# Moving one half-tile load from the sync queue to the queue of ScalarE, beside the end of a store

## The chip, the cores and the metric

The kernel runs on one core of a Trainium2 chip. The metric is the device time in microseconds of one execution. "Span" is the time from the first to the last instruction in the profile of one execution; in every timed execution below, the time is 1.7 to 1.9 us more than its span.

## The reference

It is a rotary position embedding on half of each head. `x` is 16 x 512 x 16 x 64 in float32 (33.55 MB); `cos` and `sin` are 512 x 32.

```python
x1, x2 = (x[..., :half_dim], x[..., half_dim:])          # half_dim = 32
rotated_first  = x1[..., :16] * cos[..., :16] - x1[..., 16:] * sin[..., :16]
rotated_second = x1[..., :16] * sin[..., :16] + x1[..., 16:] * cos[..., :16]
return np.concatenate([rotated_first, rotated_second, x2], axis=-1)
```

Each byte of `x` comes in once and goes out once: 67.1 MB in all.

## The kernel before

The tensor is cut into T = 4 tiles of 8.39 MB. A tile has 64 KB in each of 128 partitions, in a ring of three slots, so tile 3 must wait until tile 0 has been stored. VectorE rotates each tile in place in two halves.

```python
    ring = const_pool.tile([P, NS, K, H, D], fp32)      # NS = 3 slots, K = 16 rows of a tile per partition
    ...
    load(0)
    load(1)
    load(2, 0, KC)                                      # KC = 8: half of tile 2
    ...
    def rotate(t, lo, hi):                              # four VectorE operations: mul, mul, sub, add
        ...
    def turn(t):
        rotate(t, 0, KC)
        rotate(t, KC, K)
        return store(t)

    turn(0)                                             # rotates tile 0 and stores it
    load(2, KC, K)                                      # the other half of tile 2, behind that store
    near = load(3, 0, KL)                               # KL = 14 of 16; waits for the store to land
    load(3, KL, K)
    tc.add_manual_dep(turn(1).ins, near.ins.name, ...)  # the store of tile 1 waits for the near load
    turn(2)
    turn(3)
```

All of these transfers are issued on the sync queue (`nc.sync`). In what follows the "near load" is the first load of tile 3, the "moved load" the second half of tile 2, and a "row" the part of a transfer that lies in one partition: 64 KB for a full tile, 32 KB for a half.

## Time and profile before

| | before |
|---|---|
| time, median of the first 3 runs | 161.47 us (161.44 to 161.71) |
| span of the profiled run | 160.3 us |
| VectorE busy | 112.4 us (70%) |
| DMA engines busy | 97.8% of the span |
| bytes moved | 67.24 MB, 433 GB/s from 24 to 150 us |
| store of tile 0 issued / landed | 49.94 / 72.5 us |
| moved load issued / landed | 50.33 / 81.9 us |
| store of tile 1 issued | 98.96 us |

A DMA that is issued is not yet at work: the 16 DMA engines take its rows after those of the DMAs ahead. The page's section 6 tells the time from issue to landing. What holds an issue back stands in the waits of the sync queue (SPq). The profiled execution took 162.1 us, 0.6 more than the median of the timed ones; a second profile of the same kernel (before_again below, 161.64 us) has the store landed at 71.8 and the store of tile 1 issued at 98.47.

### The profile page before, as it was taken

To read this page: it belongs to the slowest core of one execution; us is meant where nothing else is said; L and a number is where in the kernel's file an instruction comes from. 1 tells how busy PE (TensorE), PEld (TensorE's weight loads), DVE (VectorE), ACT (ScalarE), POOL (GpSimd) and SP (SyncE) were. 2 spreads that over 40 slices of the span, in tenths; PEclk is the share of its full clock that TensorE was granted. 3 is DMA by queue.
4 is the path that set the end of the run, shared out by engine and by line. 5 is a ranking of instruction groups with operands and counts; after the bars stand their busy time and mean duration, and the time that the engine had idled before them with its cause. 6 is when DMAs were issued, how large, how long until landed. Compare 5 with 4: busy or idle time off the path is not lost.

```text
span 160.3 us, 113 instructions
## 1 busy us (share of the span) xinstructions
DVE 112.4 (70%) x43; POOL 1.4 (1%) x6
## 2 busy tenths in 40 slices
DVE  1000959999999999999999999999999950000000
POOL 3000000000000000000000000000000000000000
DMA  7969969699699996999999995996996996996990
GB/s 262 540 262 540 491 294 523 278 507 491 294 392 441 474 523 262 523 392 392 499 482 458 458 444 253 546 523 262 523 523 262 523 507 278 523 507 278 523 507 16
DMA packets 1504, 67.24 MB, mean 419 GB/s; under 512 B 192, under 2 KB 192, under 8 KB 224
## 3 DMA queue, kind: packets, MB, share of 16 engines
q1 hardware_dynamic: 1440, 67.11, 97.6%
q0 software_dynamic: 64, 0.13, 0.2%
HBM read 33.69 MB, written 33.55 MB: 419 GB/s over the span
## 4 chain that ended last, share of the span: by engine, by line
DVE 59%; DMA 14%; issue 7%; DVEq 1%
DVE b_t L96 22%; DVE ring L97 22%; DMA ring<-in_x_dram 14%; DVE ring L101 10%; DVE ring L98 4%; DVEq L148 1%; DVEq L96 0%
## 5 line engine op out<-in xcount | busy, mean ns | idle before, releaser
L96 DVE TENSOR_TENSOR b_t<-ring,table 128x4096 f32<-128x4096 f32 x8 | 35.5, 4432 | 2.1 <-DMA ring<-in_x_dram 1.9
L97 DVE TENSOR_TENSOR ring<-ring,table 128x4096 f32<-128x4096 f32 x8 | 35.4, 4424 | 0.3
L98 DVE TENSOR_TENSOR ring<-ring,b_t 128x2048 f32<-128x2048 f32 x8 | 18.3, 2287 | 0.3
L101 DVE TENSOR_TENSOR ring<-ring,b_t 128x2048 f32<-128x2048 f32 x8 | 18.2, 2280 | 0.0
L73 DVE LOAD_MASK_SELECT spun<-stage x1 | 0.0, 14 | 14.4 <-DMA stage<-in_sin_dram 14.4
L83 DVE COPY table<-packed 32x1024 f32<-32x1024 f32 x4 | 2.7, 684 | 0.1
L80 DVE COPY packed<-spun 32x512 f32<-32x512 f32 (+3 forms) x4 | 1.7, 416 | 0.1
L61 DVE MEMSET stage<- 128x512 f32 x1 | 0.5, 485 | 0.9 <-PEq L137 0.9
L73 DVE STREAM_SHUFFLE spun<-stage 128x512 f32<-128x512 f32 x1 | 0.7, 723 | 0.0
L63 POOL DMA_DIRECT2D stage<-in_cos_dram x1 | 0.6, 649 | 1.3 <-DVE stage L61 1.3
L64 POOL DMA_DIRECT2D stage<-in_sin_dram x1 | 0.5, 532 | 0.0
L137 POOL MEMSET const-float32-0.0<- 128x1 f32 x1 | 0.1, 93 | 0.2 <-issue 0.2
L137 POOL MEMSET const-bfloat16-1.0<- 128x1 bf16 x1 | 0.1, 95 | 0.0
L137 POOL MEMSET const-uint8-127<- 128x1 uint8 x1 | 0.1, 93 | 0.0
L137 POOL MEMSET const-float32-1.0<- 128x1 f32 x1 | 0.1, 92 | 0.0
## 6 DMA issues: line engine op xcount, KB each, us to landing
ring<-in_x_dram SPq DMA_DIRECT2D x2, 4096.0 KB, 41.4
ring<-in_x_dram SPq DMA_DIRECT2D x1, 7168.0 KB, 26.4
ring<-in_x_dram SPq DMA_DIRECT2D x1, 1024.0 KB, 28.5
stage<-in_cos_dram POOLq DMA_DIRECT2D x1, 64.0 KB, 9.0
stage<-in_sin_dram POOLq DMA_DIRECT2D x1, 64.0 KB, 13.4
out_dram<-ring SPq DMA_DIRECT2D x4, 25.6
ring<-in_x_dram SPq DMA_DIRECT2D x2, 32.0
```

The lines of the kernel that those rows point to most:

```text
L61: nc.vector.memset(stage[:, :, :, 0:Q], 0.0)
L63: nc.gpsimd.dma_start(out=spread[:, 0, 0], in_=cosf)
L64: nc.gpsimd.dma_start(out=spread[:, 0, 1], in_=sinf)
L73: nc.vector.stream_shuffle(out=spun[:], in_=stage.rearrange("p t k j -> p (t k) j")[:, :, 0:Q], mask=[j % PQ * REP for j in range(PB)],)
L80: nc.vector.tensor_copy(out=packed[0:n], in_=spun[q * PB : q * PB + n])
L83: nc.vector.tensor_copy(out=table[r * PB : (r + 1) * PB].rearrange("p t k c j -> p (t k) c j"), in_=packed.unsqueeze(2).to_broadcast((PB, ...
L96: nc.vector.tensor_mul(out=b_t, in0=x1, in1=s)
L97: nc.vector.tensor_mul(out=x1, in0=x1, in1=c)
L98: nc.vector.tensor_sub(out=x1[:, :, :, 0:Q], in0=x1[:, :, :, 0:Q], in1=b_t[:, :, :, Q:HF])
L101: nc.vector.tensor_add(out=x1[:, :, :, Q:HF], in0=x1[:, :, :, Q:HF], in1=b_t[:, :, :, 0:Q])
L137: nc = _bacc.Bacc("TRN2", target_bir_lowering=False, num_devices=1)
L148: with _tile.TileContext(nc) as tc:
```

## The change

The second half of tile 2 is no longer queued behind the store of tile 0. It goes on ScalarE's queue, and is released when VectorE ends the first half of tile 1, in the hope that it moves beside the last quarter of the store.

```diff
-    def load(t, lo=0, hi=K):
-        return nc.sync.dma_start(out=rows(t, lo, hi), in_=xf[t, :, lo * R : hi * R])
+    def load(t, lo=0, hi=K, queue=nc.sync):
+        return queue.dma_start(out=rows(t, lo, hi), in_=xf[t, :, lo * R : hi * R])
 ...
-    turn(0)
-    load(2, KC, K)
+    rotate(0, 0, KC)
+    rotate(0, KC, K)
+    store(0)
+
+    rest = load(2, KC, K, nc.scalar)
     near = load(3, 0, KL)
     load(3, KL, K)
+    behind(rest, rotate(1, 0, KC))      # a wait on the last operation of that half
+    rotate(1, KC, K)
 ... (the rest, the store of tile 1 behind the near load included, as before)
```

More of the change, by code (lines that the diff above doesn't have):

```diff
@@ L100, in rotate, with behind @@
         )
-        nc.vector.tensor_add(
+        return nc.vector.tensor_add(
             out=x1[:, :, :, Q:HF], in0=x1[:, :, :, Q:HF], in1=b_t[:, :, :, 0:Q]
         )
-    def turn(t):
+    def behind(transfer, point):
+        tc.add_manual_dep(
+            transfer.ins,
+            point.ins.name,
+            mybir.DependencyInfo(
+                mybir.DependencyClass.Sync, mybir.DependencyReason.DATA
+            ),
+            reason="the transfer follows others at the DMA engines",
+        )
+    rotate(0, 0, KC)
+    rotate(0, KC, K)
+    store(0)
+    rest = load(2, KC, K, nc.scalar)
+    near = load(3, 0, KL)
+    load(3, KL, K)
+    behind(rest, rotate(1, 0, KC))
+    rotate(1, KC, K)
+    behind(store(1), near)
+    for t in range(2, T):
         rotate(t, 0, KC)
         rotate(t, KC, K)
-        return store(t)
-    turn(0)
-    load(2, KC, K)
-    near = load(3, 0, KL)
-    load(3, KL, K)
-    tc.add_manual_dep(
-        turn(1).ins,
-        near.ins.name,
-        mybir.DependencyInfo(mybir.DependencyClass.Sync, mybir.DependencyReason.DATA),
-        reason="the store follows the loads at the DMA engines",
-    )
-    turn(2)
-    turn(3)
+        store(t)
 _INS = ['x', 'cos', 'sin']
```

## The prediction

> **What bounds the kernel now.** I read the head of the page first, then the DMA share, then one long window of the DMA view, then the waits.
>
> ```profile
> span 160.3 us, 113 instructions
> DVE 112.4 (70%) x43; POOL 1.4 (1%) x6
> ...
> DMA packets 1504, 67.24 MB, mean 419 GB/s; under 512 B 192, under 2 KB 192, under 8 KB 224
> ...
> q1 hardware_dynamic: 1440, 67.11, 97.6%
> q0 software_dynamic: 64, 0.13, 0.2%
> ```
>
> VectorE works 70% of the span; the DMA engines work 97.8% of it (97.6 + 0.2). The chain of the page says "DVE 59%", but it is followed back from the last instruction and does not enter the stores that end the program, so I do not take it for the bound. The test is whether the DMA engines have holes in the middle. The DMA view from 24 to 150 us:
>
> ```profile
> DMA packets 1216, 54.53 MB, mean 433 GB/s; under 512 B 128, under 2 KB 128, under 8 KB 128
> ...
> q1 hardware_dynamic: 1216, 54.53, 100.7%
> ```
>
> They have none: the packets' own durations fill 16 engines' time (the 0.7% is the edge of the window). So the kernel is bound by bytes at 433 GB/s: 67.24 MB / 433 GB/s = 155.3 us. The DMA view from 0 to 4 us shows the first packets at 1.7 us, so 157.0 us are given; the other 3.3 us of the span are the slower first rows and the landing of the last store with the end of the program. The time is 161.47 us, 1.2 over this span.
>
> From that rate: 433 / 16 = 27.06 GB/s for one engine, so a 64 KB row (65,536 bytes, one partition of a full tile) takes 2.42 us and a 32 KB row (half a tile) 1.21 us. A full tile gives each engine 8 rows, 19.4 us; a half tile 9.7 us.
>
> Now the waits of the DMA queue and of VectorE, and two lines of the timeline:
>
> ```profile
> SPq L55 <- DMA out_dram<-ring: 21.7, 1, 21.7
> ...
> DVE b_t L96 <- DMA ring<-in_x_dram: 1.9, 1, 1.9
> ...
> 49.94 0.35 SPq L58 DMA_DIRECT2D out_dram<-ring  x1
> ...
> 63.39 4.43 DVE L96 TENSOR_TENSOR b_t<-ring,table 128x4096 f32<-128x4096 f32 x1
> ```
>
> The store of tile 0 is issued at 49.94. The queue then issues the second half of tile 2 at 50.33, and is held 21.7 us for the store to land, to 72.47, before it may issue the loads of tile 3 into the same slot. VectorE waits for a load only once, for the first. In the last line VectorE starts the second half of tile 1 at 63.39: this is the point at which the changed kernel releases the load. VectorE finishes the last tile at 130.6.
>
> **What the Trainium skill says.** (1) "DMA: Bandwidth & Descriptors", section "Issuing engines are not separate DMA queues": DMAs of different issuing engines run on the same 16 DMA engines and interleave; a second issuer saves only its issue time. (2) Same page, "Queues, rings and completion order": an engine goes round-robin over the rings that have work, switching at packet boundaries, and puts a typical packet at 9 to 17 descriptors. The trace agrees with the first half and not with this length. The small table loads come by another queue while the tile loads run; the DMA view from 7 to 10.2 us shows it:
>
> ```profile
> GB/s 0 0 0 102 205 2662 3430 2509 2458 922 0 1638 0 0 0 0 0 0 0 0 0 0 0 0 0 0 0 0 0 0 0 0 0 0 0 1638 2458 4096 2458 819
> DMA packets 60, 2.03 MB, mean 635 GB/s; under 512 B 14, under 2 KB 14, under 8 KB 30
> ```
>
> Slices are 0.08 us. A small packet starts on each engine about 7.3, one 64 KB row is taken at once behind it, and the small queue's next record (4 bytes, its completion) waits for that row, to about 9.9. A tile load has 8 rows and a completion record per engine; had the engine drained those nine first, the small packets would have waited for the end of tile 0 near 22. So the switch comes after each row. (3) Same page, "Where 436 GB/s comes from": 435 GB/s is the ceiling of the 16 ports; the 433 here is that ceiling.
>
> **The change, part by part.** No byte, row or VectorE instruction is removed. One load moves from the sync queue to that of ScalarE (idle in this kernel), and waits for the first half of tile 1.
>
> Release: 63.4. The first load was issued at 0.74 and its rows began from 1.7 to 2.6, so an issue takes 1.0 to 1.9 us to reach the engines: 64.4 to 65.3. The rows of the store begin at about 52.2 plus multiples of 2.42: 64.3, 66.7, 69.1, with the end at 71.5 (and its landing at 72.47, 1.0 later). The row of 64.3 is running, so the first switch is at 66.7, with two store rows left of eight: the "last quarter".
>
> Alternation from there, L for a load row of 1.21 and S for a store row of 2.42: L to 67.9, S to 70.3, L to 71.5, S to 73.9, L to 75.1, then the completion of the store. It lands at about 76.1, 3.6 us **later** than before. The loads of tile 3 are issued there and reach the engines at 77.1 to 78.0. At 75.1 the moved load still has 5 of 8 rows, 6.0 us, so the engines have work to 81.2: 3.2 to 4.1 us of margin, no hole.
>
> Then the moved load shares the engines with the first load of tile 3, whose rows are 7/8 of 64 KB, 2.11 us. It has 2 or 3 rows left at 78 and each now waits for such a row, its completion as well: I get 88.3 to 90.6 for its landing, where before it landed at 50.33 + 31.6 = 81.9. So the load is issued 13 us later and lands some 7 us later: it is not brought forward at all. VectorE wants it at 90.28 (timeline, fifth use of L96), so a new wait of 0 to 0.5 us may show there.
>
> What it is worth at the end: the engines have moved the same bytes at the same rate by 98.1, the first load of tile 3 lands at 98.9 as before and releases the store of tile 1 as before. VectorE, even 0.5 us later, ends at 131.1; the store of tile 3 must be issued by about 139.2 - 1.9 = 137.3, since two stores of 19.3 us lie ahead from 100.5. That is 6 us of slack. Sum: 0 removed, 0 added on the path; **161.5 us**.
>
> **The rivals.**
>
> A. Read and write overlap. If a load row and a store row of different queues could run at once on an engine, the two store rows left would be hidden: 2 x 2.42 = 4.8 us, 156.6 us, 3% faster. For it: nothing in this trace has a load and a store in two queues at once. Against it: the two queues at 7 to 10 us took turns, and 433 GB/s holds for loads and stores alike, which looks like a limit of the engine itself.
>
> B. The load goes ahead of the store. If the engines favoured the new queue until empty, the load would run 66.7 to 76.4, the store's last rows to 81.2, its landing 82.2, and the loads of tile 3 would come at 83.2 to 84.1 to engines idle since 81.2: 2.0 to 2.9 us lost, 163.5 to 164.4. The turns at 7 to 10 us speak against it.
>
> C. The store goes ahead of the load (packets of nine records, as the skill's figure has it). Then the order is that of before, the store lands at 72.5, and the time is the same.
>
> D. The first DMA of ScalarE comes late. It has until 71.5, 8.1 us after its release, before engines run dry; the sync queue needed 1.0 to 1.9. Every microsecond past that is lost. Unlikely.
>
> E. Mixed rows are slower each. At 10% over the 14 us of the mixed store and load (66.7 to 81) that is at most 1.4 us.
>
> **Range and chances.** My line of argument and C both give 161.5, with executions of the kernel before spread over 161.44 to 161.71. I give these together about 85%. E in a mild form widens the upper side, so the range is 161.0 to 162.4. B and D (about 8%) give up to 164.4, mostly still within 2% (164.7). A has about 3%. So: faster 0.03, same 0.95, slower 0.02.
>
> **What the changed profile would show.** Right: a second hardware queue with 144 packets (128 rows and 16 completions) and 4.19 MB, the first with 1296; the long window still at 433 GB/s and about 100%; the wait of the sync queue for the store about 25.7 us instead of 21.7 (its start comes 0.4 earlier, as one issue is gone); the moved load about 26 us from issue to landing; the wait for the near load of tile 3 ending at 98.9 again; the last VectorE instruction between 130.6 and 131.1. Store landing still at 72.5 means C; at 82 with a drop in GB/s from 81 to 84, B; a long window above 433 GB/s and the last stores some microseconds earlier, A; a wait of L96 of several microseconds, that the moved load lost more turns than I counted. The prediction fails if engines stand idle anywhere between 24 and 150, or if 433 GB/s is not their ceiling when both directions run.

## The result and the profile after

| | before | after |
|---|---|---|
| time, median of 5 runs each | 161.55 us (161.44 to 161.71) | 161.81 us (161.72 to 161.84) |
| ratio | | 1.0014 (0.9999 to 1.0028) |
| span of the profiled run | 160.3 us | 160.1 us |
| store of tile 0 landed | 72.5 us | 74.4 us |
| moved load issued / landed | 50.33 / 81.9 us | 63.46 / 88.1 us |
| store of tile 1 issued | 98.96 us | 98.71 us |

A ratio here is the mean time of one kernel's runs over that of the other's runs of the same rounds, so it is not quite the ratio of the medians quoted.

The page of the changed kernel has the new queue:

```profile
span 160.1 us, 113 instructions
...
q1 hardware_dynamic: 1296, 62.92, 91.5%
q10 hardware_dynamic: 144, 4.19, 6.2%
q0 software_dynamic: 64, 0.13, 0.2%
```

The shares still add up to 97.9%. The DMA view from 24 to 150 us, the same window as before (columns of the queue lines: packets, MB, share of the time of 16 engines):

```profile
DMA packets 1216, 54.53 MB, mean 433 GB/s; under 512 B 128, under 2 KB 128, under 8 KB 128
...
q1 hardware_dynamic: 1072, 50.33, 92.7%
q10 hardware_dynamic: 144, 4.19, 7.9%
```

The same packets, the same bytes and the same rate as in the kernel before. Only their order differs. First the wait for the near load (the second of the pair in the line) and the issue of the store of tile 1 in the kernel before; its wait for the store, 21.7 us, stands in the prediction:

```profile
SPq L58 <- DMA ring<-in_x_dram: 46.5, 2, 25.6
...
98.96 31.98 SPq L58 DMA_DIRECT2D out_dram<-ring  x3
```

Then, in the changed kernel, the waits of the sync queue, that of VectorE, and the moved load in the timeline and in the list of DMA issues:

```profile
SPq L58 <- DMA ring<-in_x_dram: 44.4, 2, 23.4
...
SPq L55 <- DMA out_dram<-ring: 24.0, 1, 24.0
...
DVE b_t L96 <- DMA ring<-in_x_dram: 1.9, 1, 1.9
...
63.46 0.37 ACTq L55 DMA_DIRECT2D ring<-in_x_dram  x1
...
74.42 0.80 SPq L55 DMA_DIRECT2D ring<-in_x_dram  x2
...
98.71 32.31 SPq L58 DMA_DIRECT2D out_dram<-ring  x3
...
ring<-in_x_dram ACTq DMA_DIRECT2D x1, 4096.0 KB, 24.6
```

The wait for the store grew (21.7 to 24.0 us), because the store now gives turns to the load. The wait for the near load, the second of the pair in the first line, shrank by as much (25.6 to 23.4). They lie one after the other, so nothing is gained. Nor is the 0.25 us by which the store of tile 1 is issued earlier here a gain: beside before_again, whose waits are 21.0 and 25.8 us, it comes 0.24 us later. The moved load, on which the change was built, lands 6 us later than before, at 63.46 + 24.6 = 88.1, and VectorE does not notice: its only wait for a load is still the 1.9 us of the first.

How long did the moved load take to get to the engines? The DMA view from 64 to 72 us, in slices of 0.2 us:

```profile
GB/s 0 0 0 0 0 0 0 0 655 3604 328 655 0 0 0 0 0 0 0 0 0 0 819 1147 655 0 0 0 0 655 2621 983 983 0 0 0 0 0 0 0
DMA packets 48, 2.62 MB, mean 328 GB/s; under 512 B 0, under 2 KB 0, under 8 KB 0
...
q1 hardware_dynamic: 32, 2.10, 65.0%
q10 hardware_dynamic: 16, 0.52, 18.5%
```

Sixteen store rows begin near 65.8, then 16 load rows (half the bytes) near 68.4, then 16 store rows near 69.8. The first load rows came 5.0 us after the issue, and one round of store rows later than I had counted.

### The profile page after: what moved, and what is told of

Read it like the earlier page. It is cut to its first block, busy times and chain, and to the rows that moved or that the text cites. A ratio compares the mean times of both kernels' runs of the same rounds, so it can differ in the third digit from the quotient of the medians.

```text
span 160.1 us, 113 instructions
## 1 busy us (share of the span) xinstructions
DVE 112.3 (70%) x43; POOL 1.4 (1%) x6
## 4 chain that ended last, share of the span: by engine, by line
DVE 60%; DMA 14%; issue 6%; DVEq 1%
DVE b_t L96 22%; DVE ring L97 22%; DMA ring<-in_x_dram 14%; DVE ring L101 10%; DVE ring L98 6%; DVEq L155 1%; DVEq L96 0%
## 6 DMA issues: line engine op xcount, KB each, us to landing
ring<-in_x_dram ACTq DMA_DIRECT2D x1, 4096.0 KB, 24.6
```

## The experiments

Twelve runs were made, three of them of the two kernels unchanged, and all results were correct. The last column is the issue of the store of tile 1, which is when the near load has landed. It is the handiest single number of these traces: from there to the end of the span there are 61.3 to 61.4 us in every kernel below but release_late, so all that the others differ by happens before it.

| run | time, median (lowest to highest) | ratio to before of the same rounds, 95% | store of tile 0 landed | store of tile 1 issued |
|---|---|---|---|---|
| before_again | 161.58 (161.54 to 161.65) | 1.0006 (0.9993 to 1.0018) | 71.8 | 98.47 |
| after_again | 161.83 (161.71 to 162.09) | 1.0022 (1.0010 to 1.0035) | 74.7 | 98.94 |
| after_third | 161.68 (161.57 to 161.99) | 1.0011 (0.9998 to 1.0025) | 74.2 | 98.49 |
| last_store_scalar | 161.43 (161.34 to 161.56) | 0.9996 (0.9983 to 1.0010) | 71.6 | 98.36 |
| same_queue | 161.44 (161.35 to 161.79) | 0.9993 (0.9981 to 1.0006) | 71.7 | 98.65 |
| release_behind | 161.88 (161.62 to 162.03) | 1.0019 (1.0007 to 1.0031) | 71.6 | 98.83 |
| release_quarter | 162.62 (161.75 to 162.77) | 1.0050 (1.0029 to 1.0071) | 75.7 | 99.66 |
| release_mid | 162.65 (161.67 to 163.00) | 1.0055 (1.0017 to 1.0093) | 77.0 | 99.59 |
| release_early | 164.16 (163.99 to 164.35) | 1.0163 (1.0148 to 1.0178) | 81.4 | 100.83 |
| load_first | 164.82 (164.53 to 164.85) | 1.0199 (1.0184 to 1.0214) | 82.1 | 101.67 |
| release_late | 165.55 (165.26 to 165.70) | 1.0246 (1.0231 to 1.0262) | 71.4 | 96.87 |
| tables_scalar | 164.58 (164.54 to 164.97) | 1.0196 (1.0182 to 1.0210) | 77.2 | 101.44 |

My theory was that the end is set by bytes over 433 GB/s as long as no engine runs dry, so that the order of the rows is free within a margin. Rivals: load and store rows overlap, or slow each other; a second queue has a price of its own.

### Does order cost, and when?

**load_first**, on the kernel before: the load goes ahead of the store, on one queue.

```diff
-    turn(0)
     load(2, KC, K)
+    turn(0)
```

> The kernel before with the second half of tile 2 issued ahead of the store of tile 0, on the same queue: the order of rival B, made on purpose. Theory 'bytes, as long as no hole opens': the store's rows run 61.9 to 81.2, it lands at 82.2, the loads of tile 3 reach the engines at 83.2 to 84.1, the engines stand idle 2.0 to 2.9 us, and the time is 163.5 to 164.4. If order were wholly free: 161.5.

It took 164.82 us, 3.3 more than before and 0.4 over the upper end of what was expected. The DMA view from 78 to 86 us, slices of 0.2 us:

```profile
GB/s 0 0 1311 1966 1311 328 328 0 0 0 0 0 0 0 0 0 0 0 0 0 0 0 0 0 0 2580 573 860 0 287 287 0 0 0 0 0 0 0 0 2294
...
q1 hardware_dynamic: 56, 2.42, 77.4%
```

The last store rows begin at 78.4 to 79.4 and are through about 2.4 us later. Then nothing starts until 83.0: the store has to land (82.10) and the near load, which waits for it, has to be issued and reach the engines. By the packet records the engines idle for 2.1 us, and the rows right after the gap are slower, by 0.6 us per engine. The bytes are the same; the place of one load costs 2%. So order is free only while something lies behind the store.

**release_early** has the change's two queues, with the load released at the end of tile 0.

```diff
-    rotate(0, KC, K)
+    early = rotate(0, KC, K)
 ...
-    behind(rest, rotate(1, 0, KC))
+    behind(rest, early)
+    rotate(1, 0, KC)
```

> The changed kernel with the moved load released at the end of tile 0 (about 50) instead of after the first half of tile 1 (63.4), so that it takes turns with the whole store. The store lands near 81 to 82, when no or one row of the moved load is left; idle 1 to 3 us, time 162.5 to 164.5. Eight load rows beside eight store rows also test overlap: if they could run at once, the span would fall by several us instead; and if each mixed row were slower, the rate from 55 to 80 would be below 433 GB/s.

The DMA view from 55 to 79 us, slices of 0.6 us:

```profile
GB/s 1638 109 0 0 819 55 1638 109 0 0 819 55 1638 109 0 0 819 55 1638 109 0 0 819 55 1638 109 0 0 819 55 1529 218 0 0 765 109 1529 218 0 0
DMA packets 208, 10.49 MB, mean 437 GB/s; under 512 B 0, under 2 KB 0, under 8 KB 0
...
q1 hardware_dynamic: 112, 7.34, 70.7%
q10 hardware_dynamic: 96, 3.15, 30.3%
```

This is the clearest picture of two queues on one set of engines. A full tile's row, then a half tile's row of half the bytes, every 3.6 us (2.42 + 1.21), for six turns. The rate is the usual one (437 in this window, whose edges cut rows). There is no overlap of load and store rows, and no penalty per row either: rival A of the prediction and the lasting form of rival E fall together. Only the first rows of the two queues, before this window, were slow (49 to 55 us, 0.5 us per engine by the packet records). The time went to the same place as in load_first: the store landed at 81.4 when the moved load was used up (it landed at 49.73 + 31.9 = 81.6), and the engines then idled 1.8 us by the packet records.

**release_late** releases the load only after all of tile 1.

```diff
-    behind(rest, rotate(1, 0, KC))
-    rotate(1, KC, K)
+    rotate(1, 0, KC)
+    behind(rest, rotate(1, KC, K))
```

> The changed kernel with the moved load released after the whole of tile 1 (76.8), when the store of tile 0 is long out. Then nothing lies behind the store: it ends at 71.5, lands at 72.5, the loads of tile 3 arrive at 73.5 to 74.4, so the engines idle 2.0 to 2.9 us; later the moved load takes turns with tile 3 and lands near 99, 9 us after VectorE wants it, which makes VectorE end near 139.5, about when the last store can first move. Time 163.5 to 165. If the moved load were worth nothing as cover for the landing, 161.8.

It took 165.55 us, 0.5 over what was expected. The hole at 71 to 73 us is there (2.0 us by the packet records). The rest is VectorE, in the waits and in the timeline:

```profile
DVE b_t L96 <- DMA ring<-in_x_dram: 13.2, 2, 11.3
...
101.60 4.43 DVE L96 TENSOR_TENSOR b_t<-ring,table 128x4096 f32<-128x4096 f32 x1 [11.32 <-DMA ring<-in_x_dram]
```

VectorE waited 11.3 us, not 9. It ended at 141.9, and the store of tile 3 reached the engines after they had run dry again (0.6 us by the packet records). This is the one variant in which VectorE's slack, some 6 us in the prediction, was used up.

**release_mid** and **release_quarter** lie between, released after the second and the third operation of the first half of tile 1.

```diff
-        nc.vector.tensor_mul(out=x1, in0=x1, in1=c)           # release_mid
+        product = nc.vector.tensor_mul(out=x1, in0=x1, in1=c)
-        nc.vector.tensor_sub(                                 # release_quarter
+        difference = nc.vector.tensor_sub(
 ...
-    behind(rest, rotate(1, 0, KC))
+    behind(rest, rotate(1, 0, KC)[0])                         # that operation, returned by rotate
```

> The changed kernel with the moved load released at 58.8, after the second operation of tile 1, 4.6 us earlier than in the change. With 5 us to its first row it begins at about 63.8, the store lands at 76 to 78, the loads of tile 3 reach the engines at 77 to 80, and the moved load still has rows to 81.2: no hole. Time as the changed kernel, 161.6 to 161.9. It tells whether the cost between the changed kernel and release_early is a threshold (margin used up) or grows evenly with the release time; even growth would put about 0.6 us or more here.

> The changed kernel with the moved load released one operation earlier (61.15, after the subtraction of the first half of tile 1). My reading now: a load reaches the engines 1.0 to 2.0 us after its issue, and an engine has the next row of the running queue taken up already, so the first load row begins at the second row boundary: here about 65.9, with two store rows left, the quarter that the change names; store landing about 76, near load of tile 3 landing as in the changed kernel. Time 161.6 to 162.0 if only holes cost. If the cost grows evenly from the changed kernel (+0.3) to release_mid (+1.1), about 162.1. If the arrival falls on a row boundary for some engines, engines drift apart by a row as in release_mid and runs scatter up to 163.

Neither has the hole between store and near load. Yet each has runs of two kinds: release_mid 161.67 once and 162.61 to 163.00 three times; release_quarter 161.75 and 161.87, and 162.60 to 162.77 four times. Both profiles are of the slow kind. First the DMA view of release_mid from 63.3 to 65 us, then that of release_quarter from 66 to 67.5, each a window that starts at about the first load rows (the fourth store row of the first view starts at 64.97 and belongs to the next turn; the three store rows of the second start at 65.94 to 65.97, just before the window):

```profile
q10 hardware_dynamic: 13, 0.43, 65.5%
q1 hardware_dynamic: 4, 0.26, 54.9%
```

```profile
q10 hardware_dynamic: 13, 0.43, 73.7%
```

Only 13 of 16 engines took a load row at this turn; three took another store row. In the packet records these three store rows lasted 4.1 to 4.2 us instead of 2.42, in both kernels, so three engines fell behind the rest. Store rows of the turn before it were slow on all engines too, up to 3.3 us. A transfer has landed when its slowest engine is done, and the near load came about 1 us late (99.6). The quick runs of the two kernels have no profile; if they are the ones without this accident, as seems likely, the cost between the changed kernel and release_early is no slope: it is the accident of three engines in most runs of two release points, with no time that long in the 15 runs of the changed kernel, and beyond that the hole. That the release falls on a row boundary for some engines fits what is seen, but why exactly three engines, and why their row takes 1.7 us more, stays open. I had not expected the accident for release_mid, and for release_quarter only as a possibility.

### Where do the 0.2% of the changed kernel come from?

**before_again**, **after_again** and **after_third** are the two kernels unchanged.

> The kernel before, unchanged, as a control. It tells how far two copies of one kernel differ (I expect a ratio of 1.000 within 0.0015), gives the span of each timed run, and a second profile. In the first profile the rows of the load of tile 1 were slower than others, some 0.75 us in all; if that is chance it should be gone or elsewhere here; if it belongs to the kernel it comes again between 27 and 42 us.

> The changed kernel, unchanged, on the same chip as the other three. Theory 'bytes' (the end is set by bytes over 433 GB/s while no hole opens; order is free): 161.5 to 161.9, ratio 1.000 to 1.003. Again the first rows of the moved load should begin about 5 us after its issue and cost about 0.5 us per engine more than later rows. If the 0.3 us over before in the first result was chance, the ratio is under 1.001.

> The changed kernel once more, on the same chip as same_queue, so that the two stand side by side: 161.7 to 161.9, ratio 1.001 to 1.003, the store of tile 1 issued at 98.7 to 98.9.

The kernel before agrees with itself within 0.06%. The changed one came out over it three times (1.0014, 1.0022, 1.0011), though only the second interval lies above 1. Time minus span is 1.7 to 1.9 us in both, so what there is lies inside the span; and its span varies: after_third was profiled at 159.8 us, with the store of tile 1 issued at 98.49 as in before_again.

The slow rows were a trap. In the first pair of profiles the changed kernel showed slow rows at 66 to 69 us, where the load joins the store, and the kernel before did not, which looked like the price of a fresh queue. But before_again shows them too, at 68 to 71 us on its single queue: store rows of up to 3.4 us instead of 2.42 just before the first load rows, which took up to 1.8 instead of 1.21. By the packet records this came to 0.6 us per engine there, and to 0.6, 0.75 and 0.6 in the three profiles of the changed kernel. Slow rows in the load of tile 1, which the first profile of before had instead, did not come again at that size. The DMA view of the last 16 store rows, in windows of 3 us that hold nothing else, first of before (68 to 71 us), then of before_again (67 to 70):

```profile
q1 hardware_dynamic: 16, 1.05, 80.6%
```

```profile
q1 hardware_dynamic: 16, 1.05, 94.9%
```

Sixteen rows on 16 engines: the share times 3 us is the mean row, 2.42 us and 2.85.

The place of the slow rows tells nothing, but their sum does. Added up by the packet records from 20 us to the landing of the near load, time over the usual 2.42, 2.12 or 1.21 us of a row was 0.47 to 0.62 us per engine in the profiles of same_queue, last_store_scalar, before_again and after_third, and 0.74 to 0.90 in release_behind, after_again, after and the first one of before. The store of tile 1 was issued at 98.36 to 98.65 in the first four and at 98.71 to 98.96 in the others. So a profile that is a few tenths of a us late has more slow rows, and each of the two kernels has a profile in either group.

**last_store_scalar** gives the kernel before a second hardware queue without a load on it.

```diff
-    turn(3)
+    turn(3, nc.scalar)        # turn and store pass the queue on
```

> The kernel before with only its last store moved to the queue of ScalarE. The two stores that remain at 131 us then take turns; no load is near. Theory 'a second hardware queue costs a fixed time outside the span': 0.25 us over before, span as before. Theory 'the first rows of a fresh queue are slow': the span grows by up to 0.5 us and slow rows show about 5 us after the issue at 130.6. Theory 'load and store rows beside each other are slow': neither, as both are stores; ratio 1.000. Theory 'bytes' alone: ratio 1.000 to 1.003.

The ratio is 0.9996. The two last stores took turns and cost nothing, and no time was added outside the span: a second queue was free here. The store was issued at 130.6, and its first rows began near 136.2, all at 2.42 us by the packet records: slow rows do not come with a fresh queue as such.

**same_queue** keeps the late release and puts the load back on the sync queue.

```diff
-    rest = load(2, KC, K, nc.scalar)
+    rest = load(2, KC, K)
```

> The changed kernel with the moved load back on the sync queue, its release kept at 63.4. So it is issued 13 us later than in the kernel before, while the store runs, but follows the store on one queue. Rivals for the 0.2 to 0.3 us of the changed kernel and of release_behind: if the queue of its own costs it, this one gives 0.999 to 1.001 and issues the store of tile 1 at 98.3 to 98.5; if it is the arrival of a load while a store runs, whatever the queue, this one gives 1.0015 to 1.003 and 98.7 to 98.9.

Its ratio is 0.9993, next to 1.0011 of after_third on the same chip. The two profiles do not bear the difference out: same_queue issued the store of tile 1 at 98.65, outside both ranges that were expected, and after_third at 98.49, earlier than its own. **release_behind** keeps ScalarE's queue but takes no turns with the store, being released after the first operation of the second half of tile 1.

```diff
-    behind(rest, rotate(1, 0, KC))
-    rotate(1, KC, K)
+    rotate(1, 0, KC)
+    behind(rest, rotate(1, KC, K)[0])     # its first operation, returned by rotate
```

> The changed kernel with the moved load released later, after the first operation of the second half of tile 1 (67.8). It arrives at 68.8 to 69.8, when each engine runs or has taken up the last row of the store, so on its own queue it follows the store as it did in the kernel before: no turns are taken. If the 0.2% of the changed kernel comes from taking turns with the store, it is gone here: ratio 0.999 to 1.001, store landed at 71.7 to 72. If it comes from a second queue or from a load that arrives beside a running store at all, it stays: 1.002. If the engines hold more rows ahead than one, or fewer, a short hole at 71 would show.

The store landed at 71.6, so no turns were taken, and the ratio is 1.0019 all the same. It also shows what a later landing does: the moved load shared the engines with the near load and landed at 92.4. VectorE waited for it:

```profile
DVE b_t L96 <- DMA ring<-in_x_dram: 4.0, 2, 2.1
```

VectorE ended 2.2 us later than in the kernel before (132.8), within its slack, so this is not the 0.2%. Taken together, turns with the store are not needed for it, and neither a second queue alone nor the late issue alone brought it. What is left is a load on a queue of its own at this place, perhaps by more slow rows where it joins the store (0.7 us per engine in release_behind, 0.5 in same_queue). But the intervals of same_queue and after_third overlap, two of the four intervals of kernels with such a load include 1, and a single profile of each cannot tell how often slow rows come. So neither this cause nor the 0.2% itself is shown.

### A queue that is not fresh, and a surprise

**tables_scalar** is the changed kernel with the table loads also on ScalarE's queue.

```diff
-    nc.gpsimd.dma_start(out=spread[:, 0, 0], in_=cosf)
-    nc.gpsimd.dma_start(out=spread[:, 0, 1], in_=sinf)
+    nc.scalar.dma_start(out=spread[:, 0, 0], in_=cosf)
+    nc.scalar.dma_start(out=spread[:, 0, 1], in_=sinf)
```

> The changed kernel, with the two small table loads moved from GpSimd's queue to that of ScalarE, so that this queue has been used 60 us before the moved load. If slow first rows belong to a fresh queue, the moved load should begin 1.0 to 2.4 us after its issue here (one row earlier: store of tile 0 landing near 76 instead of 74.4) and without slow rows. If they belong to mixing load and store rows, or to a queue that has been idle, they stay as in the changed kernel. Time 161.3 to 161.9 either way.

As to its question: the moved load was issued at 66.28 and its first rows began near 71.3, again 5.0 us later and with slow rows. A used queue is not quicker. The time was a miss of 3 us, from elsewhere. Here are its packets and the wait of VectorE for the tables, which was 14.4 us in the kernel before (its tables went by GpSimd's queue):

```profile
q10 hardware_dynamic: 240, 4.33, 6.3%
...
DVE spun L73 <- DMA stage<-in_sin_dram: 19.2, 1, 19.2
```

Of the 240 packets 144 are the moved load's, so the tables are 96, six for each engine, against 64 (four for each) on GpSimd's queue. Each waits for one 64 KB row of the loads beside it: 2 x 2.42 = 4.8 us more, and the tables did land 4.7 us later (20.4 instead of 15.7). VectorE then began later, the store of tile 0 was issued at 52.83 instead of 49.94, and the engines, done with the loads at 51.5, idled for 2.5 us. It is a hole like that of load_first at another place: there the engines wait for a landing, here for VectorE.

No run points to a version that clearly beats both kernels: the two best, same_queue and last_store_scalar, are level with the kernel before.

## Why the prediction was right, point by point

**The bound** held: 433 GB/s and full engines from 24 to 150 us in both kernels, and a cost as soon as engines idle: 3.3 us in load_first for 2.1 of idle time, 2.6 in release_early for 1.8, the rest mostly slower rows. That the 433 is a ceiling of the ports, as the prediction says, is an agreement of two numbers; no run here shows what sets it.

**Time minus span** I gave as 1.2 us. That set a median against the span of another run; the profiled run itself took 162.1 us, so it is 1.8.

**No overlap of loads and stores** (rival A) held, best seen in release_early. **Turns of one row** held, against rival C, and tables_scalar confirms it with a count of records.

**The first switch "at 66.7, with two store rows left"** is the step that was off. It came at 68.4, with one store row left. The rows began 0.75 us earlier than in the profile that I worked from, and an issue took 5.0 us to its first row. My 1.0 to 1.9 us is right for idle engines: in load_first the near load was issued at 82.10 and its rows began at 83.1 to 84.1. On engines at work, the rows of the second queue came at the second row boundary after that, in the changed kernel, in tables_scalar, in last_store_scalar and for 13 engines of release_mid and release_quarter. In release_behind, where the store had no row left at the first boundary, the load came there, 2.6 us after its issue. It looks as if an engine has its next row taken up already; this is inferred, not shown. So the load runs beside the last eighth of the store, not the last quarter.

**The landings** that follow from it: the store at 74.2 to 74.7 rather than 76.1, and the wait for it 24.0 us rather than 25.7. The moved load landed at 88.1, at the lower edge of my 88.3 to 90.6, and 6 us later than before rather than 7. The near load landed at 98.7, as reckoned to 0.2 us; that is partly luck, as profiles of one kernel differ by up to 0.5 us there (98.47 and 98.96 before). The new wait of VectorE, 0 to 0.5 us, did not show.

**The margin**, 3.2 to 4.1 us in my count, was larger still: the store landed 1.7 us earlier than I had it. It was real, as release_early, load_first and release_late have none and pay.

**The size**: I predicted 161.5 and no change; 161.81 was measured, with 1.0011 to 1.0022 in three sets. The number alone does not tell my argument from rival C, which gave the same 161.5; the turns do. Rival E had allowed for a loss of up to 1.4 us by slower mixed rows. A loss of 0.2 to 0.3 us may be there, but not from rows slow all through the turns: release_early has six turns at the full rate, and release_behind has the loss without turns. Slow rows only where load and store meet stay possible, and stay untested.

## What to carry to other kernels

When the DMA engines are full from end to end, moving a transfer to another queue or another time mostly permutes bytes (within 0.3% here, but some 0.7% in most runs of two release points); ask instead what lies behind each transfer whose landing another transfer waits for, because landing, issue and arrival needed some 2 us of cover here (2.1 idle in load_first). A load that was late anyway can be that cover, so a change that brings it forward can take the cover away and cost 2% (load_first). And a small transfer beside a stream of large rows paid one large row for each of its own records (tables_scalar, 2.42 us each).

## What the Trainium skill lacked or had wrong

- "DMA: Bandwidth & Descriptors", "Queues, rings and completion order": the typical packet of 9 to 17 descriptors is not the unit of turns here. Two sync/scalar queues changed turns after every record of the trace, 64 or 32 KB (release_early, a pair every 3.6 us), completions included (in the changed kernel that of the store waits for a load row, to 73.6).
- Same page, "Specifications": about 0.6 us to the first byte on the sync and scalar path. From issue to the first row of each engine, idle engines needed 1.0 to 2.0 us (load_first).
- No page tells what that becomes on busy engines: 5.0 us in the changed kernel, at the second row boundary after it; 2.6 us in release_behind, where the other queue had run out of rows.
- Same page, "Issuing engine by pattern": sync and scalar are called generally faster than GpSimd. The table loads landed 4.7 us later on ScalarE's queue than on GpSimd's, with six records per engine instead of four beside 64 KB rows.
- No page has the slow rows where a stream changes from store to load, 0.6 us per engine in before_again and none in the first profile of before.
